# Gate values v by row blocks with both column halves, plain weights, an opening in program order, and unread matmuls ahead of the first operand

## The chip, the cores and the metric

The kernel runs on one core of a Trainium2 chip. The metric is the device time of one execution in microseconds (us); a kernel's time is the median of its runs. A difference of 0.2% (2.8 us) is about what a measurement of this kernel tells from no change.

## The reference, cut to what matters

```python
mod = jnp.einsum("bd,de->be", c_act, w_ada[l]) + b_ada[l]
shift, scale, gate = jnp.split(mod, 3, axis=-1)
h = rms_norm(x, norm_g[l]) * (1.0 + scale[:, None, :]) + shift[:, None, :]
z = jnp.einsum("bsd,de->bse", h, w_in[l])
a, a_glu, a_gate, u, v, b_gate = jnp.split(z, SPLITS, axis=-1)
y_a = conv_group(a, a_glu, a_gate, ...)
y_b = gmlp_group(u, v, b_gate, ...)
```

One layer, 2048 positions, 1024 channels, float32. `h` is needed by every product, and `h` needs the modulation (`shift`, `scale`), which is a product of `c_act` with 1024 x 2048 values of `w_ada`, and the RMS of every row of `x`. `v` is one 1024-column block of `z`; its LayerNorm statistics are needed before the gMLP group.

## The kernel before, in words

The 2048 positions are done in two halves of 1024 (`hf`); all of `h` for a half lies in SBUF. Every float32 operand is split into a high part (written by ScalarE, line 133 or 254) and a low part (written by VectorE, line 134 or 255), and a product is three matmuls: high by high, high by low, low by high. The `a`, `u` and `s` columns use a Strassen scheme (`unit`, `product`) on seven blocks of `h`, among them `A11`, `A12`, `A22` and the sums `S1` to `S4`. `v` has no such scheme: it is 384 matmuls of 128 x 512 a half, from lines 326 to 328.

`h` comes in four chunks `k` of 128 channels, each with a partner `k + 4`. Row block `r` is 512 positions, column half `g` 512 columns of `v`. For one `k`, `mod_block` (line 187) multiplies two 128 x 1024 tiles `wa` of `w_ada` with `c` and sums them on VectorE, and this is done for `k` and `k + 4`; `h_scale` (line 245) scales `x` by it and by the row's reciprocal RMS; `h_parts` splits the result. The reciprocal RMS is made by `x_rows0`: squares on ScalarE, a sum over chunks on VectorE (line 216), a sum over partitions on TensorE (`pc_x`), a square root, and a spread over the partitions through a matmul (`pr_x`, line 163).

`v_half` goes over the column halves outside and, within each, over both row blocks in an interleaved list of (r, k). Row block 0 takes `A11` and `A12` with the weights B1 and B2; row block 1 takes `S1` = A21 + A22 with B1 and `A22` with Bd = B2 - B1, which gives the same sum. `v_ops` splits three weight tiles of each k and g, and `keep` stores them in DRAM for the second half. A scheduler puts the instructions of each engine in order from the dependences, except VectorE up to the first chunk, which follows the program (`manual_schedule`). An engine runs its instructions in order, so one that waits holds all behind it; that holds for the queue of DMA issues on SP too. Results of `v` lie in eight PSUM banks (`bank` six, `xbank` two); `act(v, ps...)` (line 335) moves a bank out, line 339 squares it for the statistics.

Of the kernel before, what the change touches and what calls it, by code (L numbers as in the profile page):

```python
# [39 lines left out]
def hybrid_layer_kernel(  # L40
# [933 lines left out]
```

## Time and profile before

| | |
|---|---|
| three runs | 1404.55, 1405.76, 1407.66 us, median 1405.76 us |
| profiled execution, its own time | 1404.41 us |
| its span, first to last instruction | 1401.5 us |
| TensorE matmul busy | 97% of the span |
| VectorE, ScalarE busy | 84%, 41% |

A line of the profile names the source line (L326), the engine (PE is TensorE, PEld its weight loads, DVE VectorE, ACT ScalarE, POOL GpSimd, SP the DMA queue of SyncE), what is written and what is read. Matmuls are pipelined, so the distance between two starts says more than the duration of one.

### The profile page before, as it was taken

The numbers are of one execution on the slowest core, as the hardware profiler recorded it, in microseconds if no ns is written. First come the engines' busy times: TensorE is split into PE (matmuls) and PEld (weight loads), VectorE is DVE, ScalarE is ACT, GpSimd is POOL, SyncE is SP. The second block draws the span as 40 slices with busy tenths as digits, with TensorE's granted clock in tenths as the row PEclk, the third lists the DMA queues.
The fourth block names the chain that finished last, engine by engine and source line by source line (L and its number), as shares of the span: only waits on it lengthen the run. The fifth ranks groups of instructions, "written<-read, shape, count | busy, mean of one in ns | idle before, by whom it ended". The sixth has DMA issues, their size and how long they took to land.

```text
span 1401.5 us, 17779 instructions
## 1 busy us (share of the span) xinstructions
PE 1354.6 (97%) x6036; PEld 1116.3 (80%) x6036; DVE 1171.6 (84%) x2000; ACT 575.8 (41%) x1099; POOL 33.6 (2%) x82
## 2 busy tenths in 40 slices
PE   4799999999999999999999999999989999999997
PEld 2578888888888888888888888888868888888886
DVE  7947599999999999798889799796987976488885
ACT  5356544344454533353212234233222345264562
POOL 0000000000000000000000000000000000000000
PEclk9799999999999999999999999999989999999999
DMA  9569788788898878676867899999888426826742
GB/s 353 215 227 343 290 280 303 281 315 312 296 335 281 330 288 331 223 252 231 269 228 249 287 356 400 381 365 378 317 330 304 169 105 207 313 84 204 246 154 102
DMA packets 137548, 383.15 MB, mean 273 GB/s; under 512 B 14641, under 2 KB 49617, under 8 KB 133362
## 3 DMA queue, kind: packets, MB, share of 16 engines
q1 hardware_dynamic: 129442, 350.28, 69.4%
q0 software_dynamic: 6144, 24.93, 4.9%
q10 hardware_dynamic: 1872, 6.82, 1.3%
q8 instruction: 47, 0.77, 0.2%
q14 instruction: 43, 0.35, 0.1%
HBM read 222.06 MB, written 159.91 MB: 273 GB/s over the span
## 4 chain that ended last, share of the span: by engine, by line
PE 94%; DVE 4%; DMA 1%; issue 1%; ACT 0%; SPq 0%; DVEq 0%; ACTq 0%
PE pq_u L388 9%; PE pq_a L388 9%; PE po L623 8%; PE po L625 8%; PE po L624 8%; PE pt_u L388 6%; PE pp_u L388 6%; PE pt_a L388 6%; PE pp_a L388 6%; PE pq_s L388 5%; PE pv L328 4%; PE pv L327 4%; PE pv L326 4%; PE pt_s L388 3%; PE pp_s L388 3%; PE px L512 2%
## 5 line engine op out<-in xcount | busy, mean ns | idle before, releaser
L460 DVE SCALAR_TENSOR_TENSOR acc<-gc,cw_sb,acc 128x496 f32<-128x496 f32 (+1 forms) x496 | 344.3, 743 | 0.7 <-ACT acc L473 0.2
L623 PE MATMUL po<-wr,y 128*128 128x512 f32 x512 | 202.9, 397 | 6.8 <-DMA wr<-dW_o 6.8
L624 PE MATMUL po<-wr,y 128*128 128x512 f32 x512 | 201.5, 394 | 0.0
L625 PE MATMUL po<-wr,y 128*128 128x512 f32 x512 | 199.7, 392 | 0.0
L460 DVE SCALAR_TENSOR_TENSOR acc<-gc,cws,acc 128x496 f32<-128x496 f32 (+1 forms) x240 | 179.4, 748 | 21.6 <-ACT acc L469 17.6
L623 PEld LDWEIGHTS po<-wr,y 128*128 128x128 f32 x512 | 96.8, 189 | 28.7 <-DMA wr<-dW_o 7.3
L624 PEld LDWEIGHTS po<-wr,y 128*128 128x128 f32 x512 | 96.8, 189 | 21.7 <-issue 1.2
L625 PEld LDWEIGHTS po<-wr,y 128*128 128x128 f32 x512 | 96.8, 189 | 20.5
L388 PE MATMUL pt_u<-H_S,w_u_M 128*128 128x512 f32 x384 | 94.0, 392 | 0.0
L388 PE MATMUL pq_u<-H_S,w_u_M 128*128 128x512 f32 x384 | 93.8, 391 | 0.0
L388 PE MATMUL pq_a<-H_S,w_a_M 128*128 128x512 f32 x384 | 92.8, 389 | 0.0
L388 PE MATMUL pt_a<-H_S,w_a_M 128*128 128x512 f32 x384 | 92.6, 390 | 0.0
L388 PE MATMUL pp_a<-H_A,w_a_M 128*128 128x512 f32 x384 | 92.6, 389 | 0.0
L388 PE MATMUL pp_u<-H_A,w_u_M 128*128 128x512 f32 x384 | 92.6, 390 | 0.0
L388 PEld LDWEIGHTS pp_a<-H_A,w_a_M 128*128 128x128 f32 x384 | 72.1, 188 | 15.0
L388 PEld LDWEIGHTS pq_a<-H_S,w_a_M 128*128 128x128 f32 x384 | 72.0, 188 | 14.9
L388 PEld LDWEIGHTS pp_u<-H_A,w_u_M 128*128 128x128 f32 x384 | 71.9, 188 | 14.9
L388 PEld LDWEIGHTS pt_a<-H_S,w_a_M 128*128 128x128 f32 x384 | 71.9, 188 | 14.8
L388 PEld LDWEIGHTS pq_u<-H_S,w_u_M 128*128 128x128 f32 x384 | 71.6, 188 | 14.5
L388 PEld LDWEIGHTS pt_u<-H_S,w_u_M 128*128 128x128 f32 x384 | 71.4, 188 | 14.5
L326 PE MATMUL pv<-wv_B,H_A 128*128 128x512 f32 x128 | 50.6, 416 | 10.9 <-ACT wv_B L133 6.8
L500 ACT ACTIVATE vc<-vc,vstat 128x128 f32<-128x128 f32 x128 | 51.1, 482 | 21.7 <-DMA vc<-dV 19.7
(232 smaller groups left out, 2310.5 us busy)
## 6 DMA issues: line engine op xcount, KB each, us to landing
dW_o<-ws SPq DMA_DIRECT2D x16, 1024.0 KB, 7.5
wr<-dW_o SPq DMA_DIRECT2D x16, 1024.0 KB, 8.6
wa<-in_wa_ss_dram SPq DMA_DIRECT2D x16, 512.0 KB, 7.3
dW_B<-wv_B SPq DMA_DIRECT2D x16, 512.0 KB, 5.0
dV<-v SPq DMA_DIRECT2D x32, 256.0 KB, 3.8
vc<-dV SPq DMA_DIRECT2D x16, 512.0 KB, 5.3
raw_a<-in_w_main_dram SPq DMA_DIRECT2D x16, 512.0 KB, 5.9
dG<-g SPq DMA_DIRECT2D x16, 512.0 KB, 5.6
```

Of the source, the lines that this page charges most:

```text
L326: nc.tensor.matmul(ps[r][t], a0, s[:, 0, :], start=st, stop=False)
L327: nc.tensor.matmul(ps[r][t], a0, s[:, 1, :], start=False, stop=False)
L328: nc.tensor.matmul(ps[r][t], a1, s[:, 0, :], start=False, stop=sp)
L388: mm = lambda w, a, st, sp: nc.tensor.matmul(ps, w, a, start=st, stop=sp, skip_group_check=True)
L460: STT(out=pairs(acc, h), in0=pairs(g[:, i : i + n], at), scalar=tab[:, j, i : i + 1], in1=pairs(acc, h), op0=ALU.mult, op1=ALU.add,)
L500: act(vch[:, t, :], vch[:, t, :], AF.Identity, bias=vstat[:, 8 + t : 9 + t], scale=vstat[:, t : t + 1])
L512: nc.tensor.matmul(ps[:, t * P : (t + 1) * P], vch[:, 4 * b + t, :], wsj, start=True, stop=True)
L623: nc.tensor.matmul(ps, yh, hi, start=st, stop=False, skip_group_check=True)
L624: nc.tensor.matmul(ps, yh, lo, start=False, stop=False, skip_group_check=True)
L625: nc.tensor.matmul(ps, yl, hi, start=False, stop=sp, skip_group_check=True)
```

## The change

`v` is now made row block by row block, each with both column halves, in `V.step(r, k)`: 48 matmuls for one k. Row block 1 takes a new block `A21` (which lies in the tile of `S4` until `S4` is made) with B1 and `A22` with B2, so Bd, its subtraction, its split and its eight stores are gone. The weights of all four k and both g stay in SBUF in the first half: those of k = 2 and 3 in the ring of eight slots, those of k = 0 and 1 in tiles of `S1` to `S3`, which are made later. The stores of the weights move from the making of the weights to row block 1.

In the first half the chunks come in the order 2, 3, 0, 1 for row block 0 and 0, 1, 2, 3 for row block 1. VectorE for the whole of row block 0, and SP to the end of row block 1, follow the program's order. The RMS of positions 512 to 1023 no longer comes from the transposed `x`: `x_squares` loads these rows as they are, ScalarE sums their squares, VectorE takes the reciprocal root, and the result goes to DRAM (`dR`, 512 runs of 4 bytes) and back, spread over 128 partitions. `S1` to `S4` are made in `second_rows`. `keep_warm` adds 13 matmuls to a bank that nobody reads: eight of 256 columns on the chunks of `x`, four of 512 on the first weights and one on `dg_x`.

```diff
--- before.py
+++ after.py
         nc.tensor.matmul(pr[:, :n], ones, dg[:, :n], start=True, stop=True)
+        if name == "x0":
+            keep_warm(dg, n)
         nc.scalar.copy(dst, pr[:, :n])
...
-    wa_homes = [f"H_{b}_{k}" for b in ("S4", "S2", "S3") for k in range(KH) if (b, k) not in (("S2", 3), ("S3", 3))]
+    wa_homes = [f"H_{b}_{k}" for k in range(KH) for b in ("S4", "A22")] * 2
+    wv_homes = [f"H_{b}_{k}" for k in (2, 1) for b in ("S1", "S2", "S3")] + ["H_S1_3", "H_S1_0"]
+    raw_homes = ["H_S2_0", "H_S3_0"]
...
+        acc = rows[:, :NG]
+        pc = xbank("pc_x")
         for k in range(KC):
-            q = acc if k == 0 else flat(slot(f"q{b}_{k}"))[:, :NG] if b == 0 else ek(f"q{b}_{k}")[:, :NG]
-            act(q, xs[k][:, sl], AF.Square)
+            keep_warm(xs[k], NG // 2)
+            q = flat(slot(f"q_{k}"))[:, :NG] if k else acc
+            act(q, xs[k][:, :NG], AF.Square)
             if k:
                 TT(out=acc, in0=acc, in1=q, op=ALU.add)
-        pc = xbank(f"pc_x{b}")
         for s in range(4):
             nc.tensor.matmul(pc[:, s : s + 1], acc[:, s * P : s * P + P], ones[:, 0:1], start=True, stop=True)
-        yield
-        var = sm(f"var_x{b}", 4)
+        for g in range(2):
+            for r in raws[V_ORDER[0][0][0], g]:
+                keep_warm(r, NG)
+        mod_half(V_ORDER[0][0][0], 0)
...
+        spread(rstd_of(var, 4, "x0", fill=fill), NG, acc, "x0", sq)
...
+    def x_squares(rows):
+        ss = sm("ssx0", 4)
+        xr = []
+        for t in range(4):
+            name = f"xr0_{t}"
+            xr.append(hpool.tile([P, D], F32, tag=("H_S2_0", "H_S3_0")[t], name=name) if t < 2 else ek(name))
+            nc.sync.dma_start(xr[t], x[NG + t * P : NG + (t + 1) * P, :])
+
+        def rest():
+            for t in range(4):
+                act(xr[t], xr[t], AF.Square, accum_out=ss[:, t : t + 1])
+            TS(out=ss, in0=ss, scalar1=1.0 / D, scalar2=EPS, op0=ALU.mult, op1=ALU.add)
+            r = rstd_of(ss, 4, "x01")
+            line = dt_("dR", [4, P])
+            nc.sync.dma_start(line.rearrange("s p -> p s"), r)
+            nc.sync.dma_start(rows[:, NG:], line.rearrange("s p -> (s p)").partition_broadcast(P))
+
+        return rest
...
+        if "A2" in which:
+            plain("A21", q[1][0], sh[0])
+            plain("A22", q[1][1], sh[1])
         if "S1" in which:
             s1 = ct(f"s1_{k}")
             STT(out=s1, in0=q[1][0], scalar=sh2[:, k : k + 1], in1=q[1][1], op0=ALU.add, op1=ALU.add)
             summed("S1", s1)
-            plain("A22", q[1][1], sh[1])
...
+        if "S4" in which:
+            summed("S4", q[0][1])
...
-        H[b, k] = hpool.tile([P, 2, NG], F32R, tag=f"H_{b}_{k}", name=f"H_{b}_{k}")
+        tag = f"H_{'S4' if b == 'A21' else b}_{k}"
+        H[b, k] = hpool.tile([P, 2, NG], F32R, tag=tag, name=f"H_{b}_{k}")
...
+    def v_load(k, g):
+        n = V_ORDER[0][0].index(k)
+        if n % 3 == 0:
+            raw = [ct(f"rv{i}_{k}_{g}") for i in range(2)]
+        else:
+            if n == 1:
+                t = hpool.tile([P, D], F32, tag=raw_homes.pop(0), name=f"rv_{k}_{g}")
+            else:
+                t = ek(f"rv_{k}_{g}")
+            raw = [t[:, :NG], t[:, NG:]]
+        for i in range(2):
+            nc.sync.dma_start(raw[i], w_v[g, 2 * i + k // 2][:, (k % 2) * NG : (k % 2 + 1) * NG])
+        return raw
+
+    def v_ops(k, g, raw=None):
+
+        if raw is None:
+            out = [slot(f"wv_{t}_{k}_{g}") for t in ("B1", "B2")]
+            for t, s in zip(("B1", "B2"), out):
                 nc.sync.dma_start(flat(s), dW[t, k, g])
             return out
-        raw = [ct(f"rv{i}_{k}_{g}") for i in range(2)]
-        for i in range(2):
-            nc.sync.dma_start(raw[i], w_v[g, 2 * i + k // 2][:, (k % 2) * NG : (k % 2 + 1) * NG])
-        out = ss()
+        name = lambda i: f"wv{i}_{k}_{g}"
+        if k in V_ORDER[0][0][:2]:
+            out = [slot(name(i)) for i in range(2)]
+        else:
+            out = [hpool.tile([P, 2, NG], F32R, tag=wv_homes.pop(0), name=name(i)) for i in range(2)]
         for i in range(2):
             split(out[i], raw[i])
-        TT(out=raw[1], in0=raw[1], in1=raw[0], op=ALU.subtract)
-        split(out[2], raw[1])
-        for t, s in zip(names, out):
-            keep((t, k, g), s)
         return out
 
-    V_USE = ((("A11", 0), ("A12", 1)), (("S1", 0), ("A22", 2)))
-
-    def v_half(hf):
-
-        sums, sqs = sm(f"vsum_{hf}", 16), sm(f"vsq_{hf}", 16)
-        ws = {}
-        for g in range(2):
-            ps = {}
-            for n, (r, k) in enumerate(((0, 0), (0, 1), (1, 0), (0, 2), (1, 1), (0, 3), (1, 2), (1, 3))):
-                yield
-                if k == 0:
-                    ps[r] = [(bank if 4 * r + t < 6 else xbank)(f"pv_{hf}_{r}_{t}_{g}") for t in range(4)]
-                if r == 0 and (k, g) != (0, 1):
-                    ws[k] = v_ops(hf, k, g)
-                if n == 6 and g == 0:
-                    ws[0] = v_ops(hf, 0, 1)
-                for i, (b, o) in enumerate(V_USE[r]):
-                    s = ws[k][o]
-                    st, sp = (k, i) == (0, 0), (k, i) == (KH - 1, 1)
+
+    V_ORDER = (((2, 3, 0, 1), (0, 1, 2, 3)), ((0, 1, 2, 3), (2, 3, 0, 1)))
...
+        def step(self, r, k):
+            hf = self.hf
+            first, last = k == V_ORDER[hf][r][0], k == V_ORDER[hf][r][-1]
+            if r and not hf:
+                for g in range(2):
+                    for t, s in zip(("B1", "B2"), self.ws[k, g]):
+                        keep((t, k, g), s)
+            if first:
+                self.ps = [[(bank if 4 * g + t < 6 else xbank)(f"pv_{hf}_{r}_{t}_{g}") for t in range(4)] for g in range(2)]
+            for g in range(2):
+                if (k, g) not in self.ws:
+                    self.ops(k, g)
+                for i in range(2):
+                    s, h = self.ws[k, g][i], H[f"A{r + 1}{i + 1}", k]
+                    st, sp = first and i == 0, last and i == 1
                     for t in range(4):
-                        a0, a1 = (H[b, k][:, q, t * P : (t + 1) * P] for q in range(2))
-                        nc.tensor.matmul(ps[r][t], a0, s[:, 0, :], start=st, stop=False)
-                        nc.tensor.matmul(ps[r][t], a0, s[:, 1, :], start=False, stop=False)
-                        nc.tensor.matmul(ps[r][t], a1, s[:, 0, :], start=False, stop=sp)
...
+                        a0, a1 = (h[:, q, t * P : (t + 1) * P] for q in range(2))
+                        nc.tensor.matmul(self.ps[g][t], a0, s[:, 0, :], start=st, stop=False)
+                        nc.tensor.matmul(self.ps[g][t], a0, s[:, 1, :], start=False, stop=False)
+                        nc.tensor.matmul(self.ps[g][t], a1, s[:, 0, :], start=False, stop=sp)
+                if r or (hf and k in V_ORDER[1][0][:2]):
+                    del self.ws[k, g]
+                if last:
+                    self.evict(r, g)
+            if last and r:
+                v_stats(hf, self.sums, self.sqs)
...
+    idle = bank("idle")
+
+    def keep_warm(src, n):
+        nc.tensor.matmul(idle[:, :n], ones, src[:, :n], start=True, stop=True)
...
+    v = V(0)
+    sp_order = ExitStack()
+    sp_order.enter_context(tc.manual_schedule(engines={mybir.EngineType.SP}))
...
+        loads(("wa", V1[1]), ("wv", V1[1]))
+        x_rows0(chunks, rows0, lambda: mod_half(V1[0], 1))
+        v.ops(V1[0], 0, raws[V1[0], 0])
+        mod_block(V1[0] + KH)
+        for n, k in enumerate(V1):
+            if n:
+                mod_block(k)
+                mod_block(k + KH)
+                v.ops(k, 0, raws[k, 0])
+            h_scale(xs[k], rows0, k, B0)
+            h_parts(xs[k], k, ("A1",))
+            if n == 0:
+                loads(("wa", V1[2]), ("wv", V1[2]))
+            if n == 1:
+                loads(("wa", V1[3]), ("wv", V1[3]))
+                squares = x_squares(rows0)
+                loads(*(("x", c) for c in V2))
+            v.ops(k, 1, raws[k, 1])
+            sh2_col(k)
+            if n == KH - 1:
+                squares()
+            v.step(0, k)
...
+    def second_rows(v, xs, rows):
+        V2 = V_ORDER[v.hf][1]
+
+        for n, k in enumerate(V2):
+            h_scale(xs[k], rows, k, B1)
+            h_parts(xs[k], k, ("A2",))
+            if n:
+                h_parts(xs[V2[n - 1]], V2[n - 1], ("S1", "S2", "S4"))
+            if n == KH - 1:
+                h_parts(xs[k], k, ("S1", "S2"))
+            v.step(1, k)
+        h_parts(xs[k], k, ("S4",))
...
+            v = V(1)
+            for k in V_ORDER[1][0]:
                 h_scale(xs[k], rows1, k, B0)
                 h_parts(xs[k], k, ("A1",))
-                next(v)
-                if k:
-                    b1_block(xs, rows1, k - 1)
-                    next(v)
```

**VectorE, from the modulation of the first chunk's partner to the first scaled `x`.** `wa_4` and `wa_6` are the partner's modulation tiles, `rv` raw weights, `x0` the operand. Before:

```order
L187 SCALAR_TENSOR_TENSOR wa_4_0_189,pm_4_244<-wa_4_0_189,c_row_150 128x1024
L187 SCALAR_TENSOR_TENSOR wa_4_1_191,pm_4_244<-wa_4_1_191,c_row_150 128x1024
L134 TENSOR_TENSOR wv0_B1_0_0_268<-rv0_0_0_264,wv0_B1_0_0_268 128x512
L134 TENSOR_TENSOR wv0_B2_0_0_269<-rv1_0_0_265,wv0_B2_0_0_269 128x512
L190 TENSOR_TENSOR mod_104<-pm_4_244,bss_sb_98 128x2
L216 TENSOR_TENSOR rows0_151<-rows0_151,q1_1_388 128x512
L299 TENSOR_TENSOR rv1_0_0_265<-rv1_0_0_265,rv0_0_0_264 128x512
L191 SCALAR_TENSOR_TENSOR gsc_105<-mod_104,cols_sb_96 128x1
L245 SCALAR_TENSOR_TENSOR x0_0_171<-x0_0_171,gsc_105,rows0_151 128x512
L205 TENSOR_TENSOR sh2_106<-mod_104 128x1
L216 TENSOR_TENSOR rows0_151<-rows0_151,q1_2_391 128x512
L245 SCALAR_TENSOR_TENSOR x0_0_171<-x0_0_171,gsc_105,rows0_151 128x512
```

Now, from the diagonal `dg_x0` on:

```order
L156 TENSOR_TENSOR dg_x0_278<-ident_101,r1_x0_269 128x512
L134 TENSOR_TENSOR wv0_2_0_284<-rv0_2_0_189,wv0_2_0_284 128x512
L134 TENSOR_TENSOR wv1_2_0_285<-rv1_2_0_190,wv1_2_0_285 128x512
L188 SCALAR_TENSOR_TENSOR wa_6_0_193,pm_6_290<-wa_6_0_193,c_row_150 128x1024
L188 SCALAR_TENSOR_TENSOR wa_6_1_195,pm_6_290<-wa_6_1_195,c_row_150 128x1024
L191 TENSOR_TENSOR mod_104<-pm_6_290,bss_sb_98 128x2
L192 SCALAR_TENSOR_TENSOR gsc_105<-mod_104,cols_sb_96 128x1
L268 SCALAR_TENSOR_TENSOR x0_S3_173<-x0_S3_173,gsc_105,rows0_151 128x512
L268 SCALAR_TENSOR_TENSOR x0_S2_174<-x0_S2_174,gsc_105,rows0_151 128x512
L278 SCALAR_TENSOR_TENSOR H_A11_2_297<-x0_S3_173,mod_104,H_A11_2_297 128x512
L278 SCALAR_TENSOR_TENSOR H_A12_2_300<-x0_S2_174,mod_104,H_A12_2_300 128x512
L134 TENSOR_TENSOR wv0_2_1_317<-rv0_2_1_197,wv0_2_1_317 128x512
```

The weights' low parts moved ahead of the modulation, and the sums of squares of the other rows (`q1_...`) and the weights' difference (L299) no longer stand between it and the scaling of `x`.

**ScalarE, at the first eviction of `v`.** `v_0_r_t_g` is a bank moved out, `vj` its squares, H_A21 and H_A22 high parts of row block 1. Before:

```order
L335 ACTIVATE v_0_0_0_0_646,vsum_0_258<-pv_0_0_0_0_260 128x512
L335 ACTIVATE v_0_0_1_0_652,vsum_0_258<-pv_0_0_1_0_261 128x512
L339 ACTIVATE vj_0_0_0_645,vsq_0_259<-v_0_0_0_0_646,vnm_0_0_649 128x512
L335 ACTIVATE v_0_0_2_0_658,vsum_0_258<-pv_0_0_2_0_262 128x512
L335 ACTIVATE v_0_0_3_0_664,vsum_0_258<-pv_0_0_3_0_263 128x512
L339 ACTIVATE vj_0_0_0_645,vsq_0_259<-v_0_0_1_0_652,vnm_0_1_655 128x512
L133 ACTIVATE H_S1_2_674<-s1_2_672 128x512
L339 ACTIVATE vj_0_0_0_645,vsq_0_259<-v_0_0_2_0_658,vnm_0_2_661 128x512
```

Now:

```order
L387 ACTIVATE v_0_0_0_0_645,vsum_0_202<-pv_0_0_0_0_324 128x512
L387 ACTIVATE v_0_0_1_0_651,vsum_0_202<-pv_0_0_1_0_325 128x512
L387 ACTIVATE v_0_0_2_0_657,vsum_0_202<-pv_0_0_2_0_326 128x512
L387 ACTIVATE v_0_0_3_0_663,vsum_0_202<-pv_0_0_3_0_327 128x512
L391 ACTIVATE vj_0_0_0_644,vsq_0_203<-v_0_0_0_0_645,vnm_0_0_648 128x512
L277 ACTIVATE H_A21_0_724<-x0_0_171,mod_104 128x512
L391 ACTIVATE vj_0_0_0_644,vsq_0_203<-v_0_0_1_0_651,vnm_0_1_654 128x512
L387 ACTIVATE v_0_0_0_1_694,vsum_0_202<-pv_0_0_0_1_328 128x512
L277 ACTIVATE H_A22_0_727<-x0_0_171,mod_104 128x512
L277 ACTIVATE H_A21_1_796<-x0_1_172,mod_104 128x512
L391 ACTIVATE vj_0_0_0_644,vsq_0_203<-v_0_0_2_0_657,vnm_0_2_660 128x512
L387 ACTIVATE v_0_0_1_1_700,vsum_0_202<-pv_0_0_1_1_329 128x512
```

The high parts of row block 1 now stand among the evictions; the second bank of column half 1 (`v_0_0_1_1`) stands twelfth.

**TensorE, where row block 1 starts.** `pv_0_r_t_g` is a PSUM bank. Before, row block 1 had four banks of its own:

```order
L326 MATMUL pv_0_1_0_0_441<-wv0_B1_0_0_268,H_S1_0_435 128x512
L327 MATMUL pv_0_1_0_0_441<-wv0_B1_0_0_268,H_S1_0_435 128x512
L326 MATMUL pv_0_1_1_0_442<-wv0_B1_0_0_268,H_S1_0_435 128x512
L327 MATMUL pv_0_1_1_0_442<-wv0_B1_0_0_268,H_S1_0_435 128x512
L326 MATMUL pv_0_1_2_0_443<-wv0_B1_0_0_268,H_S1_0_435 128x512
L327 MATMUL pv_0_1_2_0_443<-wv0_B1_0_0_268,H_S1_0_435 128x512
L326 MATMUL pv_0_1_3_0_444<-wv0_B1_0_0_268,H_S1_0_435 128x512
L327 MATMUL pv_0_1_3_0_444<-wv0_B1_0_0_268,H_S1_0_435 128x512
```

Now the eight banks of row block 0 are taken over:

```order
L371 MATMUL pv_0_1_0_0_738<-wv0_0_0_502,H_A21_0_724 128x512
L372 MATMUL pv_0_1_0_0_738<-wv0_0_0_502,H_A21_0_724 128x512
L371 MATMUL pv_0_1_1_0_739<-wv0_0_0_502,H_A21_0_724 128x512
L372 MATMUL pv_0_1_1_0_739<-wv0_0_0_502,H_A21_0_724 128x512
L371 MATMUL pv_0_1_2_0_740<-wv0_0_0_502,H_A21_0_724 128x512
L372 MATMUL pv_0_1_2_0_740<-wv0_0_0_502,H_A21_0_724 128x512
L371 MATMUL pv_0_1_3_0_741<-wv0_0_0_502,H_A21_0_724 128x512
L372 MATMUL pv_0_1_3_0_741<-wv0_0_0_502,H_A21_0_724 128x512
L371 MATMUL pv_0_1_0_1_742<-wv0_0_1_516,H_A21_0_724 128x512
L372 MATMUL pv_0_1_0_1_742<-wv0_0_1_516,H_A21_0_724 128x512
L371 MATMUL pv_0_1_1_1_743<-wv0_0_1_516,H_A21_0_724 128x512
L372 MATMUL pv_0_1_1_1_743<-wv0_0_1_516,H_A21_0_724 128x512
```

The eleventh matmul of row block 1 writes the bank that the twelfth ScalarE row above empties.

## Rows read from the trace of the kernel before

**Rows 1.** The page: TensorE's busy tenths in 40 slices of the span.

```profile
PE   4799999999999999999999999999989999999997
```

**Rows 2.** Waits of TensorE to 150 us: total us, times, longest.

```profile
PE pc_x L219 <- DVE rows L216: 11.3, 2, 6.9
PE pv L326 <- ACT wv_B L133: 6.8, 1, 6.8
```

**Rows 3.** Stretches, all instructions: busy us and count of each engine, clock, DMA share, GB/s.

```profile
0.00:140.00 140.00, 108.73 (x420) 84.70 (x421) 102.24 (x205) 71.43 (x147) 3.34 (x13) 0.94 0.76 285
20.00:30.00 10.00, 5.88 (x15) 4.54 (x15) 10.00 (x20) 6.71 (x12) 0.00 (x0) 1.00 1.04 406
50.00:60.00 10.00, 5.25 (x12) 3.80 (x12) 10.00 (x17) 4.47 (x7) 0.00 (x0) 0.51 0.28 102
```

**Rows 4.** The same to 140 us for pv alone: TensorE, weight loads, ScalarE.

```profile
0.00:140.00 140.00, 95.73 (x384) 76.86 (x384) 10.38 (x32) 0.94 0.76 285
```

**Rows 5.** TensorE in order of time: start, us, line, operation, idle before it.

```profile
24.26 0.79 PE L326 MATMUL pv<-wv_B,H_A 128*128 128x512 f32 x1 [4.12 <-ACT H_A L254]
...
26.98 0.63 PE L326 MATMUL pv<-wv_B,H_A 128*128 128x512 f32 x1
27.41 0.63 PE L327 MATMUL pv<-wv_B,H_A 128*128 128x512 f32 x1
...
46.84 1.12 PE L163 MATMUL pr_x<-dg_x,ones 128*128 128x512 f32 x2 [0.23 <-DVE dg_x L156]
...
69.20 0.39 PE L326 MATMUL pv<-wv_B,H_S 128*128 128x512 f32 x1
...
79.85 0.39 PE L328 MATMUL pv<-wv_B,H_A 128*128 128x512 f32 x1
82.79 0.50 PE L326 MATMUL pv<-wv_B,H_S 128*128 128x512 f32 x1 [2.55 <-ACT H_S L133]
```

**Rows 6.** VectorE in order of time.

```profile
12.13 0.69 DVE L216 TENSOR_TENSOR rows<-rows,q 128x512 f32<-128x512 f32 x1
...
16.12 0.16 DVE L190 TENSOR_TENSOR mod<-pm,bss_sb 128x2 f32<-128x2 f32 x1
16.32 0.16 DVE L191 SCALAR_TENSOR_TENSOR gsc<-mod,cols_sb 128x1 f32<-128x1 f32 x1
...
17.25 0.69 DVE L156 TENSOR_TENSOR dg_x<-ident,r_x 128x512 f32<-128x512 f32 x1
...
20.15 1.29 DVE L134 TENSOR_TENSOR wv_B<-rv,wv_B 128x512 fp32r<-128x512 f32 x2
...
22.70 0.74 DVE L245 SCALAR_TENSOR_TENSOR x<-x,gsc,rows 128x512 f32<-128x512 f32 x1
...
28.98 1.22 DVE L187 SCALAR_TENSOR_TENSOR wa<-wa,c_row 128x1024 f32<-128x1024 f32 x1
...
30.12 1.22 DVE L187 SCALAR_TENSOR_TENSOR wa<-wa,c_row 128x1024 f32<-128x1024 f32 x1
...
49.37 2.73 DVE L245 SCALAR_TENSOR_TENSOR x<-x,gsc,rows 128x512 f32<-128x512 f32 x4
```

**Rows 7.** ScalarE in order of time.

```profile
17.07 1.33 ACT L133 ACTIVATE wv_B<-rv 128x512 fp32r<-128x512 f32 x2 [1.89 <-DMA rv<-in_w_v_dram]
...
23.48 0.72 ACT L254 ACTIVATE H_A<-x,mod 128x512 fp32r<-128x512 f32 x1
...
78.23 0.60 ACT L335 ACTIVATE v<-pv 128x512 f32<-128x512 f32 x1 [6.42 <-PE pv L328]
...
78.97 0.60 ACT L335 ACTIVATE v<-pv 128x512 f32<-128x512 f32 x1
...
79.56 0.71 ACT L339 ACTIVATE vj<-v,vnm 128x512 f32<-128x512 f32 x1
```

**Rows 8.** Tile dV from 60 to 160 us: issue to landing.

```profile
DMA to landing us min/median/max: 2.0/2.1/6.4
```

**Rows 9.** Tile cols_sb (24 KB in runs of 192 B): issue to landing.

```profile
DMA to landing us min/median/max: 5.6/5.6/5.6
```

More of the change, by code (lines that the diff above doesn't have):

```diff
@@ new lines, in v_ops, with __init__, ops, evict @@
+        return out
+    V_ORDER = (((2, 3, 0, 1), (0, 1, 2, 3)), ((0, 1, 2, 3), (2, 3, 0, 1)))
+    class V:
+        def __init__(self, hf):
+            self.hf, self.ws = hf, {}
+            self.sums, self.sqs = sm(f"vsum_{hf}", 16), sm(f"vsq_{hf}", 16)
+        def ops(self, k, g, raw=None):
+            self.ws[k, g] = v_ops(k, g, raw)
+        def step(self, r, k):
[13 more added lines that the diff above has]
+                    st, sp = first and i == 0, last and i == 1
+                    for t in range(4):
+                        a0, a1 = (h[:, q, t * P : (t + 1) * P] for q in range(2))
[8 more added lines that the diff above has]
+                v_stats(hf, self.sums, self.sqs)
+        def evict(self, r, g):
+            hf = self.hf
+            junk = sq(f"vj_{hf}_{r}_{g}")[:, :NG]
+            for t in range(4):
+                c = 8 * g + 4 * r + t
+                v = ct(f"v_{hf}_{r}_{t}_{g}")
+                act(v, self.ps[g][t], AF.Copy, accum_out=self.sums[:, c : c + 1])
+                nc.sync.dma_start(dV[hf][4 * r + t].rearrange("p j d -> p (j d)")[:, g * NG : (g + 1) * NG], v)
+                nm = sm(f"vnm_{hf}_{c}", 1)
+                TS(out=nm, in0=self.sums[:, c : c + 1], scalar1=-1.0 / NG, scalar2=None, op0=ALU.mult)
+                act(junk, v, AF.Square, bias=nm, accum_out=self.sqs[:, c : c + 1])
@@ L341, in v_half, with v_stats @@
+    def v_stats(hf, sums, sqs):
         m = vstat[:, 8:16]
@@ L706, in x_load @@
             nc.sync.dma_start(xs[k][i][:, sl], xT[k + i * KH][:, hf * T + sl.start : hf * T + sl.stop])
+    V1, V2 = V_ORDER[0]
     xs = x_home(0)
[L709 removed]
+    for k in V1:
         x_load(0, xs, k, B0)
[L711 to L722 removed]
@@ L723, in b1_block @@
-    def b1_block(xs, rows, k):
-        h_scale(xs[k], rows, k, B1)
-        h_parts(xs[k], k, ("S1",))
-    v = v_half(0)
-    next(v)
-    next(v)
-    for k in range(KH):
-        x_load(0, xs, k, B1)
-    r1 = x_rows0(chunks, rows0, 1)
-    for k in range(1, KH):
-        mod_block(k)
-        mod_block(k + KH)
-        sh2_col(k - 1)
-        h_scale(xs[k], rows0, k, B0)
-        h_parts(xs[k], k, ("A1",))
-        next(v)
-        if k == 1:
-            next(r1)
-            next(r1, None)
-        b1_block(xs, rows0, k - 1)
-        next(v)
@@ L746, in hybrid_layer_kernel, with loads @@
-    sh2_col(KH - 1)
-    b1_block(xs, rows0, KH - 1)
-    next(v)
-    for k in range(KH):
-        next(v)
-        h_parts(xs[k], k, ("S2",))
-        next(v, None)
+    k = V1[0]
+    for i in range(2):
+        wa_tile(k, i)
+    raws = {(k, 0): v_load(k, 0)}
+    for i in range(2):
+        wa_tile(k + KH, i)
+    raws[k, 1] = v_load(k, 1)
+    def loads(*what):
+        for kind, k in what:
+            if kind == "wa":
+                for c in (k, k + KH):
+                    for i in range(2):
+                        wa_tile(c, i)
+            elif kind == "wv":
+                for g in range(2):
+                    raws[k, g] = v_load(k, g)
+            else:
+                x_load(0, xs, k, B1)
@@ new lines, in hybrid_layer_kernel @@
+    chunks = [xs[k][i] for k in V1 for i in range(2)]
+    idle = bank("idle")
[4 more added lines that the diff above has]
+    sp_order.enter_context(tc.manual_schedule(engines={mybir.EngineType.SP}))
+    with tc.manual_schedule(engines={mybir.EngineType.DVE}):
+        loads(("wa", V1[1]), ("wv", V1[1]))
[20 more added lines that the diff above has]
+            v.step(0, k)
+        nc.vector.tensor_copy(out=cws, in_=cw_sb[:, :, :HT])
+        TT(out=cws[:, :, : W - HT], in0=cws[:, :, : W - HT], in1=cw_sb[:, :, HT:], op=ALU.add)
+        TS(out=cw_sb[:, :, HT:], in0=cw_sb[:, :, HT:], scalar1=-1.0, scalar2=None, op0=ALU.mult)
```

65 lines of the change are left out of this document (9 added, 56 removed).

## The prediction

> **What bounds the kernel now.** I read the page first: TensorE is busy in nine tenths or more of nearly every slice, and only the first two slices, some 70 us, are half empty [rows 1]. So TensorE is the bound, and there is little to win except at its start. Then I read who TensorE waits for in the first 150 us: a sum on VectorE (11.3 us in two waits, one before the first product and one of some 4.4 us after it) and a split weight (6.8 us) are the large ones [rows 2]. VectorE shows why: it is busy for the whole of 20 to 30 us and of 50 to 60 us, while TensorE is busy for 5.9 and 5.3 us [rows 3]. In the opening, then, TensorE is fed by VectorE, and what counts is in which order VectorE does its work.
>
> How much is lost: from 0 to 140 us TensorE has 420 matmul records, of which 384 are `v` [rows 3, 4], 24 are small ones of the opening (the spread of `c`, `pc_x`, `pr_x`) and 12 the first product of the next unit. At the steady distance of (79.85 - 69.20) / 47 = 0.2266 us [rows 5], 396 matmuls take 89.7 us. So **50.3 us** of the first 140 are lost. Only part is idle. The first product starts at 24.26 us, and its matmuls stand 0.43 us apart, twice the steady distance [rows 5]: they run at the lower of the two clocks, 1.2 GHz, after TensorE had idled 4.12 us. Between 50 and 60 us, around the 6.8 us wait, the granted clock is 0.51, the same lower level [rows 3]. The column shows 1.00 from 20 to 30 us, where the distances say otherwise, so I go by distances. After 82.79 us the first half of `v` has no further wait [rows 2, 5].
>
> **The change part by part.**
>
> *Until the first product.* The chain to `dg_x` holds the same steps: last sum at 12.13, two halves of a modulation, `dg_x` at 17.25 us [rows 6]. ScalarE now has a weight split ahead of the square root; that weight is in its 13th quarter megabyte (8 pieces of `x`, two `wa` of two quarters, then `rv`). Before, it came as the 17th, and ScalarE got it at 17.07 us [rows 7]; at the 406 GB/s of this stretch [rows 3] four quarters fewer are 2.6 us less, so 14.5 us, and the root is not late for 16.4 us. Hence `dg_x` at 17.25 as before. Then VectorE does two weight subtractions at 0.60 us each (1.29 us for two, less the overlap) and one `mod_block`: two halves 1.14 us apart, and two small ones 0.20 us apart with as much around them, 2.7 us together [rows 6]. That makes 17.25 + 0.60 + 1.2 + 2.7 = 21.7 us for the first scaling, which was at 22.70 because sums of the other rows stood in between [rows 6]. From there to the first product it took 24.26 - 22.70 = 1.56 us, through the ScalarE split at 23.48 [rows 5, 7]. **First product at 23.3 us.** The unread matmuls stand ahead of it: the last three start after `pr_x`, each as long as `pr_x` at the higher clock, 1.12 us [rows 5], so they end near 22.5 us and delay nothing; at the lower clock they would end some 3 us later.
>
> *Clock.* Whether the unread matmuls hold the higher clock, no row shows; what it is worth, the rows do: 12 first matmuls at 0.43 instead of 0.2266 us are 2.5 us. A gap of 2.55 us at 80 us left the clock high (the next distances are steady again), one of 6.8 us did not [rows 5, 2]. The gaps left ahead of the first product are about 2 us, nearer to the first. I take the higher clock and keep 2.5 us as the bound.
>
> *Row block 0.* One k gives TensorE 48 x 0.2266 = 10.9 us. VectorE for one k: two `mod_block` 5.4, four weight subtractions 2.4, two scalings 1.3 (four take 2.73 with overlap [rows 6]), two low parts 1.3 and some 0.3 of waiting for ScalarE: 10.7 us. So each next operand comes just in time; if VectorE needed 0.3 us more per k, the cost would be about 1 us in all. The loads: 14 MB until the last weight, at 406 GB/s some 35 us plus the start, by 40 us, where VectorE wants the last `mod_block` at 47 us. Row block 0 ends at 23.3 + 43.5 = 66.8 us.
>
> *The other rows' RMS.* VectorE is through with row block 0 at 21.7 + 3 x 10.7 + 4.1 = 58 us. The root takes 1.3 us, as an estimate from the steps before `dg_x`. Then a store and a load through DRAM, one after the other. The cheapest landing near is 2.0 us, the dearest 6.4 [rows 8], and one in short runs took 5.6 [rows 9]. Together that bounds the pair by 4 and 12 us; I take 6, near the median of 2.1 us each, since these rows are from a stretch with a queue like this one, and add for the short runs. So the scales are there at 65.3 us (63 to 71), and the first product of row block 1 could start 1.6 us later, at 66.9: no wait, at worst 6 us. The Trainium skill (DMA: Bandwidth & Descriptors, Specifications) says that a transfer under 512 B does read-modify-write, so the 4-byte runs of the store are the case it warns of; by it the pair would stand, as an estimate, at its upper bound, and the time at 1387 us. The rows show no store in such runs.
>
> *Change of row block.* Column half 0 has its last matmul 20 before the end, at 62.3 us. ScalarE then moves banks at 0.74 us each and squares at 0.7 to 0.8 [rows 7]. By its new order: four banks until 65.4, one square, H_A21 until 66.9; TensorE starts row block 1 at 67.0. ScalarE goes on with a square, a bank, two high parts, a square, and the bank that the eleventh matmul needs: 71.3 us. TensorE is there at 67.0 + 10 x 0.2266 = 69.3. **A wait of 2.0 us**; bounds 0 and, with the scales late, 6 in all with the wait above. Behind it nothing else is late: the high parts of all k stand ahead of their use.
>
> *Row block 1 and after.* 43.5 us more, to 66.8 + 0.2 + 2.0 + 43.5 = 112.5 us. The Bd work (eight subtractions, eight splits) is off VectorE, the sums S1 to S4 have some 8 us of VectorE work a k under 10.9 us of TensorE, and S4 of the last k is wanted only in the fifth product. The first unit's raw weights now stand on SP behind 16 stores of 0.52 MB, which can start when the last bank of row block 0 is moved out, near 78 us: 8.4 MB at 406 GB/s last until 99, the raw weights until 104, and they are wanted split at 112.5. Eight microseconds of cover; at the mean rate of 285 GB/s [rows 3] some 3 us would show.
>
> *Second half.* Same matmuls; before, its slices are full [rows 1], and the four bank moves (3.8 us with one square between) fit in the 5.4 us of the first 24 matmuls of row block 1. Nothing taken; 0 to 3 us.
>
> *Sum.* Lost after: 112.5 - 384 x 0.2266 = 25.5 us, against 50.3: **24.8 us less**. Everything behind is the same chain moved forward. The profiled execution took 1404.41 us, so 1379.6; the median of the runs is 1.35 us above it, so **1381.0 us**.
>
> **Rivals.** (a) *The change of row block is dearer*: the scales come at 71 us, or the raw weights late, 4 to 9 us; for it speak the short runs and the full SP queue, against it the covers above. 1385 to 1390 us. 20%. (b) *The unread matmuls do not do what they are for*: the clock is low at the first product, 2.5 us, or they delay it by 3. 1383.5 us; the gain from the order stands. 14%. (c) *Slower*: the second half's weights. Each k wants four tiles of 0.52 MB, 2.1 MB, at 406 GB/s 5.2 us plus some 2 of landing, 7.2 us. If the ring gave no room to load ahead, each of the six loads would show in full: 43 us, 1424 us; from four of six (29 us) the kernel is slower than before. Against it: eight slots hold two k's, and 7.2 us fit under 10.9. 4%. (d) *Given back*: VectorE, busy for 84% of the span, becomes the bound in the units and the gain shrinks to nothing, 1405 us. Against it, TensorE's slices are full from the third to the twenty-ninth [rows 1], so it hardly waits for VectorE there now, and VectorE's work moves forward together with TensorE's. 3%.
>
> **How the numbers follow.** The forecast itself, 1376 to 1385, has 57%; gains above 30 us (cheaper start, no wait at the change) 2%. Range 1376 to 1390: the forecast and rivals (a) and (b), with little more than 1 in 10 outside. Faster by over 0.2% (2.8 us): 0.94; the same: 0.02; slower: 0.04.
>
> **What would show it.** Right: first product at 23 to 24 us with distances of 0.23 us, no wait over 1 us inside row block 0, one of about 2 us before the eleventh matmul of row block 1, the first unit's product near 112 us. Wrong: distances of 0.43 us after 23 us (clock), a wait of TensorE for H_A21 behind the landing of `rows` (the pair of transfers), for a `w_a` weight at 112 us (the stores), or waits for weights in the second half's `v` (rival c).

## The result, and the profile of the changed kernel

The changed kernel takes **1392.22 us** (median of 4 runs, 1389.81 to 1393.25), the kernel before 1406.71 beside it; the ratio is 0.9896, 95% interval 0.9876 to 0.9915. It is faster by about 1.0%, as forecast in sign; but 1381.0 us was forecast, and 1392.2 lies 2 us above the range.

The page, TensorE's tenths in 40 slices (against [rows 1]), and TensorE's waits to 150 us (total us, times, longest; against [rows 2]):

```profile
PE   8989999999999999999999999999979999999997
```

```profile
PE pv L371 <- ACT H_A L277: 7.4, 1, 7.4
...
PE pr_x L163 <- DVE dg_x L156: 0.7, 1, 0.7
```

The two large waits are gone. One of 7.4 us has come, for a split of row block 1, and the third slice of the page shows it. The stretches (busy us and count of TensorE, weight loads, VectorE, ScalarE, GpSimd; granted clock, DMA share, GB/s; against [rows 3]):

```profile
0.00:140.00 140.00, 128.57 (x508) 99.60 (x509) 98.67 (x206) 76.55 (x163) 3.35 (x13) 0.94 0.78 295
20.00:30.00 10.00, 10.00 (x35) 6.50 (x34) 9.73 (x20) 5.03 (x8) 0.00 (x0) 0.90 1.04 392
50.00:60.00 10.00, 10.00 (x46) 8.24 (x45) 9.30 (x24) 3.01 (x7) 0.00 (x0) 1.00 0.36 126
60.00:70.00 10.00, 7.53 (x34) 5.90 (x32) 0.47 (x3) 3.12 (x10) 0.00 (x0) 0.99 0.04 3
70.00:80.00 10.00, 5.03 (x12) 3.98 (x13) 6.59 (x13) 5.80 (x14) 0.00 (x0) 0.50 0.46 176
```

From 20 to 60 us TensorE and VectorE are both full: the opening now does what it should. From 60 to 70 us VectorE works 0.47 us and the DMA engines are at 0.04, and from 67.5 us on TensorE waits too (74.97 - 7.44): for something that is neither work nor bytes. TensorE in order of time (against [rows 5]) shows the two ends of this:

```profile
23.69 0.50 PE L371 MATMUL pv<-wv,H_A 128*128 128x512 f32 x1
24.03 0.39 PE L372 MATMUL pv<-wv,H_A 128*128 128x512 f32 x1
24.26 0.39 PE L371 MATMUL pv<-wv,H_A 128*128 128x512 f32 x1
...
27.46 0.39 PE L371 MATMUL pv<-wv,H_A 128*128 128x512 f32 x1
...
74.97 0.80 PE L371 MATMUL pv<-wv,H_A 128*128 128x512 f32 x1 [7.44 <-ACT H_A L277]
...
76.00 0.63 PE L371 MATMUL pv<-wv,H_A 128*128 128x512 f32 x1
76.42 0.63 PE L372 MATMUL pv<-wv,H_A 128*128 128x512 f32 x1
...
79.83 0.53 PE L372 MATMUL pv<-wv,H_A 128*128 128x512 f32 x1
...
121.04 2.88 PE L442 MATMUL pp_a<-H_A,w_a_M 128*128 128x512 f32 x12
```

The first product starts at 23.69 us and its matmuls are 0.23 us apart: the higher clock. After the 7.4 us of waiting they are 0.43 us apart (the lower clock of the two, and 0.50 in the window's column). VectorE, ScalarE and the two transfers (issues: KB, us from issue to landing) show what was waited for:

```profile
60.00 0.16 DVE L149 SCALAR_TENSOR_TENSOR r_x<-t_x,r_x 128x4 f32<-128x4 f32 x1
...
73.41 2.08 DVE L268 SCALAR_TENSOR_TENSOR x<-x,gsc,rows 128x512 f32<-128x512 f32 x3 [9.61 <-DMA rows<-dR]
```

```profile
74.20 0.72 ACT L277 ACTIVATE H_A<-x,mod 128x512 fp32r<-128x512 f32 x1 [8.72 <-DVE x L268]
...
78.03 0.58 ACT L387 ACTIVATE v<-pv 128x512 f32<-128x512 f32 x1
```

```profile
rows<-dR SPq DMA_DIRECT2D x1, 256.0 KB, 3.9
dR<-r_x SPq DMA_DIRECT2D x1, 2.0 KB, 9.2
```

Row block 1's 512 factors are ready at 60.2 us, the 2 KB store of them lands 9.2 us after its issue, the load behind it 3.9 us after its own: VectorE goes on at 73.41. That is 13.2 us where the forecast took 6. The DMA engines' tenths in 40 slices of 58 to 70 us show that the store's packets are through by 61.6 us, in the twelfth slice; the other 7.8 us to its landing pass with the engines empty:

```profile
DMA  0000000120430000000000000000000000000000
```

ScalarE stands still meanwhile with H_A at the head of its queue, and the bank moves of row block 0 stand behind it.

**The account at the end of half 0's `v`.** The first product of the next unit starts at 121.04 us; before it was at 137.3 (it starts where the last matmul of `v`, 0.23 us earlier, has passed):

```profile
L388 PE MATMUL pp_a<-H_A,w_a_M x384: 388/389/396, 137.3 to 770.7; 128*128 128x512 f32 x192
```

So 16.3 us are won there, 24.8 were forecast. The 8.5 between them: first product 0.4 late, row block 0 0.3 longer, wait 7.4 instead of 0.2, eleven distances of (79.83 - 74.97) / 11 = 0.44 instead of 0.23 us (2.4), less the 2.0 that were taken for the eleventh matmul and did not come: 8.3. Behind `v`, 1391.0 - 121.0 = 1270.0 us follow to the end of the span, 1401.5 - 137.3 = 1264.2 before: 5.8 are given back.

### The profile page after: what moved, and what is told of

Same layout as the page of the kernel before. It is cut to its first block, busy times and chain, and to the rows that moved or that the text cites. A ratio compares the mean times of both kernels' runs of the same rounds, so it can differ in the third digit from the quotient of the medians.

```text
span 1391.0 us, 17752 instructions
## 1 busy us (share of the span) xinstructions
PE 1359.6 (98%) x6052; PEld 1117.7 (80%) x6052; DVE 1161.3 (83%) x1984; ACT 574.2 (41%) x1098; POOL 33.6 (2%) x82
## 4 chain that ended last, share of the span: by engine, by line
PE 84%; DVE 7%; DMA 4%; issue 4%; ACT 1%; SPq 0%; DVEq 0%; POOL 0%; ACTq 0%; POOLq 0%
PE pq_u L442 9%; PE po L677 8%; PE po L679 8%; PE po L678 8%; PE pq_a L442 7%; PE pt_u L442 6%; PE pp_u L442 6%; PE pt_a L442 4%; PE pp_a L442 4%; PE pq_s L442 4%; PE pv L371 3%; PE pv L372 3%; PE pv L373 3%; PE pp_s L442 3%; DVE acc L514 3%
## 5 line engine op out<-in xcount | busy, mean ns | idle before, releaser
L371 PE MATMUL pv<-wv,H_A 128*128 128x512 f32 x128 | 49.6, 403 | 7.4 <-ACT H_A L277 7.4
```

The costliest lines, as they stand in the source:

```text
L371: nc.tensor.matmul(self.ps[g][t], a0, s[:, 0, :], start=st, stop=False)
```

## The experiments

The theory: the shortfall is the late factors and the lower clock behind them (A). Rivals: VectorE's full rhythm takes back whatever is won (B); something behind `v` gives it back (C).

**1. The factors earlier.** `squares()` moves up in VectorE's order, between the two halves of the last modulation block:

```diff
-                mod_block(k + KH)
+                if n == KH - 1:
+                    mod_half(k + KH, 0)
+                    squares(lambda: mod_half(k + KH, 1))
+                else:
+                    mod_block(k + KH)
...
-            if n == KH - 1:
-                squares()
```

> The four small VectorE instructions that make row block 1's factors, and with them the store and load through DRAM, are moved up by about 6 us, between the modulation sums of the last row chunk; all else is the changed kernel. Theory A (what the forecast missed is the round trip through DRAM, 13.2 us where 6 was taken, and the lower clock that its wait left behind): the factors are stored at about 54.9 us instead of 60.2, the rows land at about 68 instead of 73.4, TensorE's 7.4 us at the change of row block become about 2, the matmuls behind it keep 0.23 us, and the time falls from 1392.2 to 1384 to 1386 us. Rival B (VectorE, with 10.7 of each 10.9 us full in row block 0, is what bounds the opening): the 1.1 us of the moved instructions push the last chunk's split back, TensorE waits there instead, and the time stays above 1389 us.

1385.65 us; ratio to before 0.9849 (0.983 to 0.9868). Its waits of TensorE, the store, and ScalarE:

```profile
PE pv L371 <- ACT v L387: 4.0, 1, 4.0
...
PE pv L371 <- ACT H_A L277: 2.0, 2, 1.5
```

```profile
dR<-r_x SPq DMA_DIRECT2D x1, 2.0 KB, 10.3
```

```profile
68.49 2.71 ACT L277 ACTIVATE H_A<-x,mod 128x512 fp32r<-128x512 f32 x4 [11.28 <-DVE x L268]
71.11 0.58 ACT L387 ACTIVATE v<-pv 128x512 f32<-128x512 f32 x1
```

The time that A expected, but not its wait: VectorE goes on at 67.71 us, 5.7 earlier, and TensorE still waits 4.0 us, now for a bank. The scheduler has here put four high parts of row block 1 ahead of all bank moves in ScalarE's order (in the changed kernel four bank moves stand first); ScalarE waits 11.28 us for the first of them, and the banks that have long been ready to move wait behind it.

**2. Runs of 16 bytes.** The rows of `x` are dealt to the partitions four neighbours each, so that the store is 128 runs of 16 bytes; the load stays one of 2 KB to all partitions:

```diff
-            nc.sync.dma_start(xr[t], x[NG + t * P : NG + (t + 1) * P, :])
+            nc.sync.dma_start(xr[t], x[NG:D, :].rearrange("(p s) d -> s p d", s=4)[t])
...
-            line = dt_("dR", [4, P])
-            nc.sync.dma_start(line.rearrange("s p -> p s"), r)
+            line = dt_("dR", [P, 4])
+            nc.sync.dma_start(line, r)
...
```

> Row block 1's rows of x are dealt to the partitions four neighbours each, so that the store of the 512 factors is 128 runs of 16 bytes instead of 512 runs of 4; the order of work and the load behind it stay. If the 9.2 us of the store go by its runs (theory A1), it takes 3 to 4 us, the rows land at about 68 us, TensorE's wait of 7.4 us shrinks to about 2 and the clock stays up: 1384 to 1386 us. If they are a latency that does not depend on the form (theory A2; the queue moved its bytes by 61.7 us, and the end came only at 69.4), the store still takes about 9 us and the time is 1392 us, within 1 us.

1384.22 us; 0.9839 (0.9819 to 0.9859). Transfers, and TensorE's waits at the change:

```profile
rows<-dR SPq DMA_DIRECT2D x1, 256.0 KB, 3.4
dR<-r_x SPq DMA_DIRECT2D x1, 2.0 KB, 2.7
```

```profile
68.34 0.50 PE L371 MATMUL pv<-wv,H_A 128*128 128x512 f32 x1 [0.50 <-ACT H_A L277]
...
73.01 1.20 PE L373 MATMUL pv<-wv,H_A 128*128 128x512 f32 x4 [1.99 <-DVE H_A L278]
```

The same bytes in another form land in 2.7 instead of 9.2 us, and the pair takes 6.1, what the forecast had taken. The matmuls stay 0.23 us apart behind both short waits (0.5 and 2.0 us), and `v` ends at 114.4 us, where the forecast had 112.5.

**3. Both.**

> The early factors and the store of 128 runs of 16 bytes together. Theory A: the pair takes 6.1 us as in the run with 16-byte runs, the rows land at about 60 us, before row block 0 ends, and the first split of row block 1 is there; what is left at the change is ScalarE's bank moves, 1 to 2 us; v of half 0 ends at 112.5 to 113.5 us (114.4 with the 16-byte runs alone, 121.0 in the changed kernel) and the time is 1382 to 1384 us. Rival B: the moved instructions delay the last chunk of row block 0 by their 1.1 us or more and no better time than 1384 comes out.

**1379.35 us** (5 runs, 1378.78 to 1381.04); 0.9808 (0.9795 to 0.982). The fastest kernel of the study, 12.9 us below the changed one and 2.7 below the lower end of what A expected. VectorE at the change, and two stretches:

```profile
60.03 2.74 DVE L268 SCALAR_TENSOR_TENSOR x<-x,gsc,rows 128x512 f32<-128x512 f32 x4 [0.39 <-DMA rows<-dR]
```

```profile
60.00:70.00 10.00, 10.00 (x46) 8.29 (x45) 9.96 (x19) 9.14 (x21) 0.00 (x0) 1.00 0.28 107
70.00:80.00 10.00, 10.00 (x45) 8.26 (x45) 7.37 (x17) 8.10 (x23) 0.00 (x0) 1.00 0.71 279
```

The factors are used at 60.03 us, 13.4 earlier, and TensorE is full through the change. All that is left of B is 0.4 us, a wait for the last chunk's split at 57 us. `v` ends at 111.5 us, 9.5 earlier than in the changed kernel. Theory A holds.

**4. Without the unread matmuls**, in the changed kernel and in that of experiment 3 (`keep_warm` does nothing):

> All matmuls whose result nobody reads are left out of the changed kernel; nothing else changes. The forecast's step: without them the first product starts at the lower clock, some eleven matmuls at 0.43 instead of 0.23 us, 2.5 us at most, 1394.5 us. Rival: TensorE is not what the opening waits for, VectorE's chunk rhythm of 10.7 us takes the loss up again within the first chunks, and the time stays at 1392 us, within 1 us; the windows will show a lower granted clock from 20 to 30 us either way.

> The same two edits, without the unread matmuls. Leaving them out of the changed kernel moved the end of v by nothing (120.9 against 121.0 us). Theory E: their gain was there and was swallowed by the later wait for row block 1's factors; with this wait gone it shows: about 2.5 us (twelve matmuls at 0.43 instead of 0.23 us) over the run with both edits. Rival F: VectorE's rhythm in row block 0 takes it up in any case: no difference, within 0.7 us.

1393.79 us (0.9906, 0.989 to 0.9922) and 1380.91 us (0.9819, 0.9806 to 0.9832): 1.6 us above its partner both times; the changed kernel's own repeat (experiment 7) differs from its first by as much. TensorE's first products in the first of the two:

```profile
23.45 0.79 PE L371 MATMUL pv<-wv,H_A 128*128 128x512 f32 x1 [3.16 <-ACT H_A L277]
24.04 0.63 PE L372 MATMUL pv<-wv,H_A 128*128 128x512 f32 x1
24.47 0.63 PE L371 MATMUL pv<-wv,H_A 128*128 128x512 f32 x1
...
29.31 0.39 PE L371 MATMUL pv<-wv,H_A 128*128 128x512 f32 x1
```

The clock is low for the first dozen, so the unread matmuls do their job. The first 16 products take 29.31 - 23.45 = 5.9 us, with the unread matmuls 27.46 - 23.69 = 3.8: 2.1 are lost. Row block 0 ends 1.8 us later, the wait for the late factors is 5.9 instead of 7.4 us, and `v` ends at 120.9 us (121.0 with them): E holds for this pair. In the second pair they take 28.72 - 23.48 = 5.2 us, 3.8 in experiment 3:

```profile
23.48 0.79 PE L371 MATMUL pv<-wv,H_A 128*128 128x512 f32 x1 [3.16 <-ACT H_A L277]
...
28.72 0.39 PE L371 MATMUL pv<-wv,H_A 128*128 128x512 f32 x1
```

So 1.5 us are lost, and 0.6 of them come back at 57 us, where TensorE now comes later and no longer waits for the last chunk's split (a distance of 0.23 us, 0.81 in experiment 3): F, in part. `v` ends at 112.1 us (111.5 with them).

**5. Unread matmuls in the new gap**: thirty of row block 0's operands, into the first bank of row block 1.

```diff
+                if not hf and r and first and not g:
+                    for _ in range(30):
+                        nc.tensor.matmul(self.ps[0][0], H["A11", k][:, 0, :P], self.ws[k, 0][0][:, 0, :], start=True, stop=True)
```

> Thirty unread matmuls (30 x 0.2266 = 6.8 us) fill TensorE's wait at the change of row block; the round trip stays late. Theory A: the wait for the first split of row block 1 still ends at 75.0 us, but the matmuls behind it are 0.23 us apart at once instead of 0.43 for twelve of them. These 2.5 us are not all won: the eleventh matmul then comes at 77.2 us, before ScalarE has moved its bank (78.6 us), and waits about 1.4 us: gain 1.1 us, 1391 us. Rival: the low rate behind the wait has another cause (operands late, the queue of instructions), and nothing changes in the distances.

1392.07 us (0.9892, 0.9876 to 0.9908): nothing won, and `v` ends at 125.7 us, 4.7 later than in the changed kernel.

```profile
75.84 0.50 PE L374 MATMUL pv<-wv,H_A 128*128 128x512 f32 x1 [1.23 <-ACT H_A L277]
76.18 0.39 PE L375 MATMUL pv<-wv,H_A 128*128 128x512 f32 x1
76.41 0.40 PE L374 MATMUL pv<-wv,H_A 128*128 128x512 f32 x1
80.51 0.80 PE L376 MATMUL pv<-wv,H_A 128*128 128x512 f32 x1 [3.70 <-DVE H_A L278]
81.11 0.63 PE L375 MATMUL pv<-wv,H_A 128*128 128x512 f32 x1
```

The distances behind the gap are 0.23 us, so the 0.43 was the clock. But the edit did more than fill the gap: the scheduler, which is free to order TensorE, now puts a matmul that needs a low part (L376) fourth in row block 1, where the changed kernel had twelve of high parts first. VectorE first scales all chunks, so the low part comes late; TensorE waits 3.7 us for it and is at the lower clock after that. Of the 4.7 us 0.9 are factors that came later (VectorE goes on at 74.28 us); the rest goes with this order, and the run does not tell what the higher clock alone is worth here. An estimate from the changed kernel: there VectorE has the low part ready at 78.84 + 0.75 = 79.6 us, and the thirteenth product, the first that needs it, starts at 80.20, so a faster TensorE could win at most 0.6 us up to there.

**6. Half 1's order**, against the loss behind `v`:

```diff
+            K = V_ORDER[hf][r]
+            todo = [(k, 0), (k, 1)]
+            if hf and r and k in K[2:]:
+                todo = [(K[2], 0)] if k == K[2] else [(k, 0), (K[2], 1), (k, 1)]
...
-                h_parts(xs[V2[n - 1]], V2[n - 1], ("S1", "S2", "S4"))
+                h_parts(xs[V2[n - 1]], V2[n - 1], ("S1", "S2") if v.hf and n == KH - 1 else ("S1", "S2", "S4"))
...
```

> The changed kernel, but in half 1's row block 1 the last two chunks run column half 0 of both first and then column half 1 of both, so that the first four banks are moved 10.9 us before v ends instead of 5.4 (the last chunk's S4 split comes after them). Theory C: the time lost again behind half 1's v (the stretch from its end to the first of the u units is 155.0 us, 151.7 before the change) is the crowd of eight bank moves at the end, whose stores hold the four small buffers that the first unit's copies need (ScalarE waits 3.1 us for a store there, and none in the kernel before): the stretch falls to about 152 us and the time to 1389 to 1390. Rival D: the stretch varies by itself (151.9 to 154.3 in the other runs), the crowd costs nothing that lasts, and the time stays within 1 us of 1392.

> The early factors, the 16-byte runs and half 1's order of the last two chunks. If theories A and C both hold, the gains add up: 2 to 3 us below the run with the two edits alone, 1380 to 1381 us; under rival D it is the same as that run, within 1 us.

1396.45 us (six runs, 1392.71 to 1401.62; 0.993, 0.9913 to 0.9947) and 1390.18 us (0.9889, 0.9876 to 0.9903): slower by 4.2 and 10.8 than the kernel that each is to be compared with. The stretch from half 1's `v` to the u units is 152.5 us in the first, as C expected, but kernels that are the same there have 151.8 to 155.8, and in the second it is 154.1 against 152.7 in experiment 3: C is not shown, and D's view that the stretch varies by itself is borne out. TensorE's waits behind it grew (in the changed kernel the first does not occur and the second is 0.9 us); the first kernel's:

```profile
PE pq_u L447 <- DVE us L476: 2.1, 1, 2.1
PE pq_s L447 <- DVE sag L476: 1.4, 1, 1.4
```

From the u units to the output products it takes 248.8 us (244.9 in the changed kernel) and 251.6 in the second. Both waits are for VectorE, whose order in half 1 the edit changed as well (the S4 split); that this is the cause was not tested by itself.

**7. The changed kernel again.**

> The changed kernel itself once more, unchanged. In its first trace 1270.0 us lie between the end of half 0's v and the end of the span, 1264.2 in the kernel before, and 1265.5 to 1271.1 in kernels that are the same there. If these 5.8 us belong to the kernel (a fixed order of work that is slower), the stretch is 1269 to 1271 us again, with waits of the first units of half 1 for a sum on VectorE; if they are chance of one execution, it comes out near the middle of the others, 1266 to 1268. The end of half 0's v should come again at 121 us, within 1 us.

1390.66 us; 0.9887 (0.9854 to 0.992). `v` ends at 121.8 us, and 1388.7 - 121.8 = 1266.9 us follow. So 3.1 of the 5.8 us did not come again. In the kernels that are the same behind `v` this stretch is 1265.5 to 1271.1 us, whether `v` ends at 111.5 or 125.7.

**8. Why the store is slow.** Four stores of 128 runs of 4 bytes (`line[s]` from `r[:, s]`), and the one store on GpSimd's queue:

> The changed kernel with the one store of 512 runs of 4 bytes cut into four stores of 128 runs of 4 bytes each, one behind the other on SP's queue. Theory G (the store's time goes by the number of runs in one transfer): each lands after about 2.7 us, as the 128 runs of 16 bytes did; with 0.4 us from issue to issue the last lands about 4 us after the first issue, the rows land at about 68.5 us instead of 73.4, and the time is 1385 to 1387 us. Theory H (it goes by the number of runs in all, which pass one after the other): the last still lands after about 9 us and the time is 1392 us, within 1 us.

> The changed kernel with the same single store of 512 runs of 4 bytes issued on GpSimd's queue instead of SP's. If the 9.2 us belong to the form of the transfer, the store takes 9 to 10 us here too and the time is 1392 us, within 1.5 us; if they belong to SP's queue and what stands in it, the store takes 3 to 5 us and the time falls to 1385 to 1388 us.

1391.28 us (0.9896, 0.9881 to 0.9911) and 1388.89 us (0.9875, 0.9859 to 0.9892). The store in each:

```profile
dR<-r_x SPq DMA_DIRECT2D x4, 0.5 KB, 9.1
```

```profile
dR<-r_x POOLq DMA_DIRECT2D x1, 2.0 KB, 8.9
```

A quarter of the runs is not faster (G falls), another queue neither. H's time came, but not its reason: the four took 9.1 us in the median, the longest 9.3, not the last alone. The second is faster than the changed kernel although its factors come no earlier (VectorE goes on at 74.20 us); `v` ends at 121.9 us, and its stretch behind `v` is 1266.7 us, as in experiment 7. Then six stores that nobody reads, behind the pair in the kernel of experiment 3 (one run, 1384.59 us, above the expected 1379 to 1382):

> The run with both edits, with six stores of the same factors behind the pair on SP's queue, which nobody reads: 128 runs of 4, 8 and 16 bytes, each kind once packed end to end and once with every run at the start of 64 bytes of its own. Theory J (the price is that of a run of 4 bytes as such): the two stores of 4 bytes land after about 9 us, those of 16 after about 2.7, whether packed or apart; 8 bytes will show where between them it turns. Theory K (the price is that of neighbouring runs of different partitions that share 64 bytes of DRAM): the packed ones of 4 and 8 bytes take about 9 us and all that stand apart about 2.7; but then the packed 16 bytes, four to 64, would have to be slow too, which the run before speaks against. Theory L (a store that is alone on the queue lands late): all six in a row land within about 3 us of their issue. The time is that of the run with both edits, 1379 to 1382 us.

```profile
dP<-r_x SPq DMA_DIRECT2D x2, 0.5 KB, 8.0
dP<-r_x SPq DMA_DIRECT2D x2, 1.0 KB, 7.5
dP<-r_x SPq DMA_DIRECT2D x2, 2.0 KB, 8.2
dR<-r_x SPq DMA_DIRECT2D x1, 2.0 KB, 2.9
```

All six land late, also those in runs of 16 bytes; the pair's own store of that form, ahead of the load, took 2.9 us. They stand behind a 256 KB load on the same queue, so the probe does not tell the forms apart, and J and K stay unproved. L's own forecast, all six within about 3 us, did not come; against L also speak the four stores in a row that took 9.1 us and the single one of 16-byte runs that took 2.7.

## Why the forecast missed

*Right.* First product at 23.3 us (23.69); the unread matmuls ran up to it here, and not to 22.5, but did not delay it, as it starts 1.55 us after the first scaling (22.14) with 1.56 forecast; distances of 0.23 us from the start; no wait in row block 0; VectorE's 10.7 us a chunk (chunks at 22.1, 32.9 and 43.6 us; 54.7 for the last, 11.2 behind, with a wait of 0.4 for ScalarE); no wait for raw weights at the first unit, nor for weights in half 1, whose `v` takes 89.8 us, 89.7 before (rival c). No full return (rival d).

*The step that failed* is the price of the pair: "I take 6, near the median of 2.1 us each, since these rows are from a stretch with a queue like this one, and add for the short runs". It took 13.2 us, above even the upper bound of 12, which was 6.4 for a landing of `dV` and 5.6 for one in runs of 192 bytes; the store alone took 9.2. With the pair at 6.1 us (experiment 2) the time is 1384.2, inside the range, and with the factors also earlier 1379.4. Of these 12.9 us 9.5 show at the end of `v` and hang on when the factors come; the rest lies behind `v`, where the changed kernel differs from its own repeat by 3.1. That 1379.4 is near the forecast of 1381.0 says little for it: it is another kernel, in which TensorE does not wait at the change of row block at all, where the forecast had 2.2 us. Rival (a) was this mechanism, with too low a price: it left out the clock behind the wait, 2.4 us, though the forecast had read just that from the kernel before, at 0.51 in [rows 3]. The Trainium skill's rule (DMA: Bandwidth & Descriptors, Specifications) that transfers under 512 B do read-modify-write pointed at the right transfer. But 16 bytes are under 512 too, and they landed in 2.7 us: the rule does not tell the two apart, the runs do.

*Two smaller terms.* The 2.0 us wait at the eleventh matmul did not come: at the lower clock TensorE was later than the bank. The 2.5 us for the unread matmuls were a bound of the price of the low clock, 2.1 and 1.5 us over the first 16 products, and not of the time: at the end of `v` nothing and 0.6 us, in the medians 1.6, which is no more than the changed kernel differs from its repeat.

*Behind `v`* "the same chain moved forward" was nearly right: 2.7 us more than in the one trace of before (experiment 7). The first output weight is waited for 8.7 us there against 6.8 before, which is most of it in that trace:

```profile
PE po L677 <- DMA wr<-dW_o: 8.7, 1, 8.7
```

```profile
PE po L623 <- DMA wr<-dW_o: 6.8, 1, 6.8
```

Why it comes later stays open.

## What to carry to other kernels

A small transfer on the path is priced from a row of its own form, and where there is none, its time is the first unknown to bound generously; choose the layout so that each partition stores its values side by side. When a late operand can head the queue of an engine that also frees banks, price what stands behind it, and price the clock behind the wait: here it was low after TensorE waits of 3.7, 4.0 and 7.4 us and high after one of 2.0. Unread matmuls held the clock, but while the operands are late a faster TensorE only waits elsewhere. And after an edit read the order of every engine again: unread matmuls in a gap moved the matmuls behind it as well.

## What was not expected of the hardware

A 2 KB store from 128 partitions took 9.2 to 10.3 us in runs of 4 bytes in the six traces that had it so on SP's queue, 8.9 on GpSimd's, and 9.1 in the median for four stores of a quarter each; in runs of 16 bytes it took 2.6 to 2.9 us in five kernels. In the changed kernel the store's packets were through by 61.6 us, 1.4 after its issue, and it landed at 69.4, so it is waiting and not bytes. Whether it is the size of the run or something that goes with it is open.
